# Half of the mixer's projection weight sums by adding loads; the reciprocal of the counts and the last operand halves at other places

## The chip, the cores and the metric

The kernel runs on one core of one Trainium2 chip. The metric is the device time of one execution in microseconds (us); a time for a kernel is the median of several runs. Profiles are of one execution each. Engines: PE is TensorE's matmul, PEld its weight load, DVE is VectorE, ACT is ScalarE, POOL is GpSimd, and SP is the sync engine, which here only issues DMAs.

## The reference: what is computed

One layer of a hybrid encoder on x (2048 positions, 1024 channels), all in float32:

```python
xn = rmsnorm(x, norm1_g)
u_pool, zq, zf, zi, zo, zg = split(xn @ w_in)           # 512 each, gates 2 x 1024
gates = sigmoid(zg + b_gate)
ya = pool_mixer(u_pool, pool_w, pool_scale) @ w_pa      # trailing means over 2, 4, 8, 16 positions
yb = hgrn2_mixer(zq, zf, zi, zo, lower_bounds, hgrn_norm_g) @ w_pb   # gated recurrence, 4 heads
x = x + (gates[0] * ya + gates[1] * yb) @ w_o
x = x + conv_glu_ffn(rmsnorm(x, norm2_g), w_up, conv_w, conv_b, w_down)
out = rmsnorm(x, final_g)
```

`pool_mixer` divides a window's sum by min(position, window), the count; only the first 16 positions have counts below the window.

## The kernel before

**Products.** Every large matrix product is done by a seven-product scheme (Strassen-Winograd) on 2 x 2 blocks: seven block products P1 to P7 instead of eight. The 2048 positions are worked in two superblocks of 1024 (b0 = 0 and 2, each two blocks of 512 positions), and a superblock's two halves are one of the 2 x 2 directions. The operand made of activations is called a form: B11, B21, T2, T1, T3, T4, B22 for P1, P2, P6, P5, P7, P4, P3. The operand made of weights is a quarter of the weight tile or a sum of quarters: P1, P2 and P4 take quarters 0, 1 and 3 as they are; P5 takes s1 = q2 + q3, P6 takes s2 = s1 + q0, P7 takes s3 = q2 + q0, and P3 takes s4 = s2 + q1 (signs are folded into the layout). Each float32 operand is split into a high part, rounded to fp32r by ACT (L231 for weights, L658 for forms), and the rest, taken by DVE (L232, L659). Three matmuls, high x high, high x low and low x high, give a product, so each P of a unit is 4 x 3 = 12 matmuls of 128 x 128 by 512 columns (L148).

**Stages of a superblock.** (1) The io stage, `proj_io`: the hgrn inputs zi and output gates zo, in the order P1, P2, P6, P5, P7, P4, P3 (products io_X to io_V; DVE's io_u of L1316 subtracts after P7 and lets P4 go on in the same PSUM bank). (2) The column projections: 14 units (`PROJ`: four fq for q and forget logits, two u for the pooling channels, eight g for the gates), each in the order P1, P6, P5, P7, P2, P4, P3. Beside them run the pool tasks and, three at a time, the hgrn tasks, whose matmuls (`pl`, `pk`, `pv`, `po`, `pt`) lie between those of the units on PE. In an hgrn task's double levels POOL copies a part of the operand (L1012), and DVE's product of L1016 reads it. (3) The branch projections pa and pb, then wo. (4) The feed-forward part, `ffn`: up (22 units), then dn.

**The weight stream.** `stream` is a list of raw loads and a list of conversions made in advance for the whole kernel. `load` (L197, SP) brings 128 x 512 floats (256 KB) into one of 8 raw buffers; `load_ahead` goes on while the buffer of eight loads ago has had its last conversion, strictly in order, and it stops at a load whose source does not exist yet. `convert` makes the two parts in one of 6 operand buffers, at most LOOKAHEAD = 4 products ahead of PE. A raw load may have a second source, `plus`, that is added on its way in: three ticks after the load (a tick is 6 large matmuls), or at the conversion if that comes first, POOL issues an adding DMA onto the same buffer (L165). It can start only when the load has landed.

**Who makes the weight sums.** In the first superblock's io stage: P5 and P6 on DVE, P7 as a load with an added load, and P3 as a load of the kept P6 sum with q1 added. For the 14 projection units of the first superblock: all four on POOL (`comb`, L444), two additions at P6, one at P7, one at P3. `keep` writes each sum to DRAM (L341, SP), and the second superblock loads them there. For wo, up and dn a background task (`prepare`) adds whole groups from DRAM to DRAM (L304, POOL; L307, ACT).

**The order of the work.** The kernel is written as tasks that are stepped every tick. A planner then orders each engine's instructions by priority (the order in which the program gives them) and by when its own simulated timeline says that they are ready; engines run their lists in order and wait at each instruction for its inputs. `behind(a, b)` holds a behind b in one engine's list. `in_turn` does so for matmuls outside the stream.

**What the change touches.** `weights_of_unit` (L433), which plans the POOL sums. `setup_task` (L601), begun at P7 of the first io stage: it makes masks on POOL, waits for the eighth adding load (`added[7]`), makes the 4 x 16 counts on POOL (L637, L641) and takes their reciprocal on DVE (L643). `forms_b_task` (L793), which makes the forms T1 to T4 and B22 of a superblock's second half; for the feed-forward part (`src[0] == "m"`) its last loop makes the four B22 halves one a tick, with the stream's lookahead at 3 instead of 4 until it ends. `mixer` (L1366), which calls `proj_io` and then joins the setup task.

Of the kernel before, what the change touches and what calls it, by code (L numbers as in the profile page):

```python
# [81 lines left out]
def tile_trunk(  # L82
# [60 lines left out]
    def join(task):  # L143
        while task.live:
            task.step()
# [22 lines left out]
    class Stream:  # L168
# [11 lines left out]
        def raw(self, src, plus=None):  # L180
            r = Raw(src, plus)
            self.raws.append(r)
            return r
# [96 lines left out]
    stream = Stream()  # L280
# [51 lines left out]
    def keep(key, t, later=False):  # L332

        nm = "kw" + "".join(str(c) for c in np.ravel(key[1])) + f"{key[0]}{key[2]}"
        kept[key] = dram.tile([P, 512], F32, tag=nm, name=nm)
        keeping.append((kept[key], t, later))
# [96 lines left out]
    def weights_of_unit(src_v, src_g, unit):  # L433
        src = quarters(src_v, src_g)
        raws, tmp = {}, {}

        def raw(i):
            if i not in raws:
                raws[i] = stream.raw(src[i])
            return raws[i]  # L440

        def comb(nm, key, x0, x1):
            t = slot(f"{nm}{key}")
            pool.tensor_tensor(t, x0, x1, ALU.add)  # L444
            tmp[key] = t
            keep(("in", unit, key), t)
            return t

        def plan(p):
            if p == "P5":  # L450
                return (lambda nm: tmp["s1"]), []
            rs = [raw(i) for i in {"P1": (0,), "P2": (1,), "P4": (3,), "P6": (0, 2, 3),
                                   "P7": (0, 2), "P3": (1,)}[p]]

            def fn(nm):
                t = [r.tile for r in rs]
                if p == "P6":
                    comb(nm, "s1", t[1], t[2])
                    return comb(nm, "s2", tmp["s1"], t[0])
                if p == "P7":  # L460
                    return comb(nm, "s3", t[1], t[0])
                if p == "P3":
                    return comb(nm, "s4", tmp["s2"], t[0])
                return t[0]

            return fn, rs

        return {p: (lambda p=p: plan(p)) for p in ORDER}
# [132 lines left out]
    def setup_task():  # L601
        scratch = [hist.rearrange("p a b -> p (a b)")[:, :64], uhist.rearrange("p a b -> p (a b)")]

        def mask_of():
            scratch.reverse()
            return scratch[0]

        keys = [(h, h, 0, h) for h in (1, 2, 4, 16)]
        keys += [(8 * h + t, 2 * h, t * h, h) for h in (4, 16) for t in range(2)]
        for key, x, off, w in keys:  # L610
            nb = 64 // x
            mf = mask_of()
            behind(pool.memset(mf, 1.0), last_root[0] if len(masks) < 6 else added[3])
            v = mf.rearrange("p (b h) -> p b h", h=x)
            pool.affine_select(out=v, in_=v, pattern=[[-2 * x, nb], [0, x]],
                               compare_op=ALU.is_ge, fill=0.0, base=-off, channel_multiplier=1)
            pool.affine_select(out=v, in_=v, pattern=[[2 * x, nb], [0, x]],
                               compare_op=ALU.is_ge, fill=0.0, base=off + w - 1,
                               channel_multiplier=-1)
            m8 = const.tile([P, 64], U8, tag=f"m{key}", name=f"m{key}")  # L620
            yield 2
            pool.tensor_copy(m8, mf)
            masks[key] = m8.rearrange("p (b h) -> p b h", h=x)
        for t in range(2):
            mf = mask_of()
            behind(pool.memset(mf, 0.0), added[3])
            pool.affine_select(out=mf, in_=mf, compare_op=ALU.not_equal, fill=1.0, base=-t,
                               pattern=[[-2, 64]], channel_multiplier=1)
            m8 = const.tile([P, 64], U8, tag=f"md{t}", name=f"md{t}")
            yield 2  # L630
            pool.tensor_copy(m8, mf)
            masks[-1 - t] = m8.unsqueeze(1)
        pool.memset(hist, 0.0)
        pool.memset(uhist, 0.0)
        while len(added) < 8:
            yield 1
        ins = pool.iota(inv[:, 3], pattern=[[1, 16]], base=1, channel_multiplier=0,  # L637
                        allow_small_or_imprecise_dtypes=True)
        behind(ins, added[7])
        for g, w in enumerate(WINDOWS):  # L640
            pool.tensor_scalar(inv[:, g], inv[:, 3], float(w), None, ALU.min)  # L641
        flat_inv = inv.rearrange("p a b -> p (a b)")
        dve.reciprocal(flat_inv, flat_inv)  # L643
        for h in range(HEADS):
            pool.memset(state[h, 0], 0.0)

# [146 lines left out]
    def forms_b_task(src, gain, forms, full, after, go, early):  # L793
# [94 lines left out]
        while len(forms["B22"]) < 4:  # L888
# [4 lines left out]
            if early:  # L893
# [6 lines left out]
                        else:  # L900
                            stream.convert()
                stream.stop = 26 + k if k < 2 else None
            yield 1
        stream.room = LOOKAHEAD

    x2d = {}
# [461 lines left out]
    def mixer(b0, forms, late):  # L1368
# [5 lines left out]
        proj_io(b0, forms, late, vd, zd)  # L1374
        if b0 == 0:
            join(setup[0])
            prep.append(Task(prepare()))


# [497 lines left out]
```

## Time and profile before

| what | value |
|---|---|
| median of 3 runs | 2542.44 us (2541.99 to 2544.25) |
| the profiled execution, time | 2540.99 us |
| its span, first to last instruction | 2539.3 us |
| mean granted clock of PE | 0.998 |
| DMA | 493.75 MB moved, mean 194 GB/s |
| conversions of weights, ACT L231 | 744, 620 ns each |
| conversions of weights, DVE L232 | 744, 749 ns each |

The profiled execution's own time is 1.45 us under the median of the runs. In the profile a group's line names the line of the kernel, the engine, the operation, what it writes and reads, the shapes and the count. A wait names the engine and line that waited, and what ended the wait. In a timeline row the first number is the start in us from the first instruction, the second the time that it took; neighbouring instructions of one kind are merged (x2), and brackets give the engine's idle time before it and what ended that.

### The profile page before, as it was taken

What the parts mean: (1) busy time and instruction counts of PE and PEld (TensorE: products, weight loads), DVE (VectorE), ACT (ScalarE), POOL (GpSimd) and SP (SyncE); (2) the same over time, 40 slices, a digit from 0 to 9 for tenths busy, and PEclk for the clock granted to TensorE, in tenths of its full rate; (3) what the DMA queues carried; (4) which work ended last, traced back from release to release, by engine and by line L of the source; (5) the groups of instructions that cost most, each with busy time, mean ns of one, the idle gap of its engine ahead of it and who ended that gap; (6) DMA issues with size and microseconds to landing.
All of it is one profiled execution on the core that took longest, in us unless ns stands there. A gap on an engine that the chain in (4) does not pass through costs nothing.

```text
span 2539.3 us, 35647 instructions
## 1 busy us (share of the span) xinstructions
PE 2511.9 (99%) x11508; PEld 2054.1 (81%) x11508; DVE 1979.2 (78%) x3508; ACT 1176.5 (46%) x2218; POOL 752.6 (30%) x1127
## 2 busy tenths in 40 slices
PE   9999999999999999999999999999999999999998
PEld 7788887788788888888888888888887888888886
DVE  7799778498999777885586778765979888778755
ACT  6434434334545444554554343442355544445534
POOL 4334343002344334461230212200033432325410
PEclk9999999999999999999999999999999999999999
DMA  8787777767898889997444343447443454447952
GB/s 274 241 200 220 201 212 227 228 214 242 209 246 240 221 233 242 264 364 243 133 146 150 107 135 109 137 150 224 149 154 110 153 154 136 150 137 236 327 165 97
DMA packets 252331, 493.75 MB, mean 194 GB/s; under 512 B 26544, under 2 KB 43056, under 8 KB 251824
## 3 DMA queue, kind: packets, MB, share of 16 engines
q1 hardware_dynamic: 184512, 313.60, 39.1%
q0 software_dynamic: 42656, 112.74, 17.6%
q10 hardware_dynamic: 24976, 65.13, 7.5%
q8 instruction: 91, 1.49, 0.3%
q14 instruction: 96, 0.79, 0.1%
HBM read 381.79 MB, written 187.17 MB: 224 GB/s over the span
## 4 chain that ended last, share of the span: by engine, by line
PE 90%; DVE 6%; issue 1%; DMA 1%; ACT 1%; POOL 0%; SPq 0%; DVEq 0%; POOLq 0%; ACTq 0%
PE dn_P L148 16%; PE up_Z L148 14%; PE up_X L148 10%; PE up_V L148 9%; PE wo_P L148 6%; PE gr_Z L148 4%; PE pb L148 4%; PE pa L148 3%; PE gr_X L148 3%; PE gr_V L148 3%; PE fr_Z L148 2%; PE io_Z L148 2%; PE fr_X L148 2%; PE fr_V L148 2%; PE io_V L148 1%
## 5 line engine op out<-in xcount | busy, mean ns | idle before, releaser
L231 ACT CAST ops<-raw 128x512 fp32r<-128x512 f32 x744 | 459.7, 620 | 823.1 <-PE dn_P L148 180.5
L232 DVE TENSOR_TENSOR ops<-raw,ops 128x512 fp32r<-128x512 f32 x744 | 554.5, 749 | 218.3 <-ACT ops L231 210.3
L1613 DVE SCALAR_TENSOR_TENSOR e<-h,cols,e 128x512 f32<-128x512 f32 x176 | 143.6, 819 | 31.2 <-ACT e L1611 24.2
L1611 ACT ACTIVATE e<-h,cols 128x512 f32<-128x512 f32 x176 | 142.6, 814 | 25.6 <-DVE h L1160 18.9
L1616 DVE SCALAR_TENSOR_TENSOR e<-h,cols,e 128x512 f32<-128x512 f32 x176 | 134.0, 770 | 2.7
L962 POOL DMA_DIRECT2D g_P<-dg_P x154 | 84.0, 547 | 159.7 <-PE dn_P L148 113.3
L1270 POOL TENSOR_TENSOR gf_P<-e,e 128x512 f32<-128x512 f32 x44 | 62.2, 1415 | 149.6 <-DVE e L1622 93.0
L1270 POOL TENSOR_TENSOR gf_P<-gf_P,e 128x512 f32<-128x512 f32 x44 | 59.0, 1341 | 72.1 <-DVE e L1622 71.6
L1606 POOL COPY h<-h 128x2 f32<-128x2 f32 x88 | 40.9, 476 | 125.0 <-DVE h L1159 118.2
L1408 POOL TENSOR_TENSOR q<-q,qs 128x512 f32<-128x512 f32 x16 | 21.7, 1358 | 187.4 <-ACT qs L1407 180.8
L1445 ACT ACTIVATE gt<-gt,cols 128x512 f32<-128x512 f32 x48 | 34.8, 725 | 85.9 <-DVE gt L1160 61.3
L1620 ACT ACTIVATE e<-e 128x512 f32<-128x512 f32 x88 | 55.6, 631 | 39.8 <-DVE e L1616 39.4
L1608 POOL COPY hist<-h 128x2 f32<-128x2 f32 x88 | 37.8, 429 | 116.6 <-DVE h L1160 114.8
L1160 DVE TENSOR_TENSOR h<-up_u,up_V 128x512 f32<-128x512 f32 x88 | 60.1, 683 | 11.3 <-PE up_V L148 10.8
L1245 DVE TENSOR_TENSOR x<-x,wo_P 128x512 f32<-128x512 f32 x88 | 56.1, 683 | 12.0 <-PE wo_P L148 11.8
L1245 DVE TENSOR_TENSOR ac<-ac,dn_P 128x512 f32<-128x512 f32 x72 | 47.1, 682 | 16.8 <-PE dn_P L148 16.6
L1012 POOL COPY qm<-q 128x64 f32<-128x64 f32 x64 | 27.1, 452 | 99.0 <-issue 26.2
L1027 PE MATMUL pl<-qm,k 128*128 128x192 f32 x256 | 50.6, 327 | 3.7 <-DVE k L1048 3.6
L1636 POOL DMA_DIRECT2D dg_P<-gf_P x88 | 50.8, 577 | 8.3 <-POOL gf_P L1270 7.4
L1195 ACT COPY up_e<-up_X 128x512 f32<-128x512 f32 x44 | 25.8, 586 | 57.8 <-PE up_X L148 52.7
L1606 POOL COPY h<-hist 128x2 f32<-128x2 f32 x88 | 46.0, 530 | 20.6 <-issue 20.6
L1027 PEld LDWEIGHTS pl<-qm,k 128*128 128x128 f32 x256 | 43.9, 189 | 9.6 <-POOL u L926 2.3
(1285 smaller groups left out, 8088.4 us busy)
## 6 DMA issues: line engine op xcount, KB each, us to landing
g_P<-dg_P POOLq DMA_DIRECT2D x154, 256.0 KB, 6.0
raw<-in_w_up_t SPq DMA_DIRECT2D x132, 256.0 KB, 3.2
raw<-in_w_in_t SPq DMA_DIRECT2D x98, 256.0 KB, 3.3
dg_P<-gf_P POOLq DMA_DIRECT2D x88, 256.0 KB, 4.0
dg_P<-e SPq DMA_DIRECT2D x66, 256.0 KB, 3.8
raw<-in_w_dn SPq DMA_DIRECT2D x66, 256.0 KB, 3.7
x<-in_x SPq DMA_DIRECT2D x64, 256.0 KB, 4.9
gd<-gt ACTq DMA_DIRECT2D x64, 256.0 KB, 3.1
```

The source lines that it names most:

```text
L148: count[1] = pe.matmul(*args, **kw)
L231: self.mark = act.copy(hi, v)
L232: low = self.low = dve.tensor_tensor(lo, v, f32(hi), ALU.subtract)
L962: eng.dma_start(t, d)
L1027: ins = pe.matmul(pa_[:, c * 192 : c * 192 + 192], ks[:, (i + c) * P : (i + c + 1) * P], mv[:, c].rearrange("p s x -> p (s x)"), start=Tru ...
L1160: return dve.tensor_tensor(dst, t, ps, ALU.add if how == "add" else ALU.subtract)
L1245: dve.tensor_tensor(t, t, ps[j], ALU.add if sg > 0 else ALU.subtract)
L1270: pin(eng.tensor_tensor(t, x0, x1, op))
L1606: pool.tensor_copy(h[:, 0:2], hist[:, mt] if hf == 0 else hs[s, 0][:, TB : TB + 2])
L1611: in_turn(act.activation(t, h[:, 2:], AF.Identity, bias=col(o_cb + mt), scale=col(o_cw + 4 * MF + mt)))
L1613: in_turn(second(dve.scalar_tensor_tensor(t, h[:, 1 : 1 + TB], col(o_cw + 2 * MF + mt), t, ALU.mult, ALU.add)))
L1616: dve.scalar_tensor_tensor(t, h[:, 0:TB], col(o_cw + mt), t, ALU.mult, ALU.add)
```

## The change

Three edits.

1. For the 14 projection units of the first superblock, s3 (P7) becomes a load of quarter 2 with quarter 0 added on its way in, and s4 (P3) a load of the s2 that was kept in DRAM, with quarter 1 added. s1 and s2 stay on POOL. The two sums are still kept in DRAM, now from the raw buffer and behind the conversion. A unit then has six raw loads instead of four.
2. The reciprocal of the counts leaves the setup task and is issued by `mixer` after the io stage, behind the last conversion's low part.
3. For the feed-forward part, the last B22 halves are issued without a tick between them.

```diff
@@ weights_of_unit
         def plan(p):
             if p == "P5":
                 return (lambda nm: tmp["s1"]), []
-            rs = [raw(i) for i in {"P1": (0,), "P2": (1,), "P4": (3,), "P6": (0, 2, 3),
-                                   "P7": (0, 2), "P3": (1,)}[p]]
+            if p == "P7":
+                rs = [stream.raw(src[2], src[0])]
+            elif p == "P3":
+                rs = [stream.raw(lambda: kept.get(("in", unit, "s2")), src[1])]
+            else:
+                rs = [raw(i) for i in {"P1": (0,), "P2": (1,), "P4": (3,), "P6": (0, 2, 3)}[p]]
 
             def fn(nm):
                 t = [r.tile for r in rs]
                 if p == "P6":
                     comb(nm, "s1", t[1], t[2])
                     return comb(nm, "s2", tmp["s1"], t[0])
-                if p == "P7":
-                    return comb(nm, "s3", t[1], t[0])
-                if p == "P3":
-                    return comb(nm, "s4", tmp["s2"], t[0])
+                if p in SUM_OF:
+                    keep(("in", unit, SUM_OF[p]), t[0], True)
                 return t[0]
@@ setup_task
         for g, w in enumerate(WINDOWS):
             pool.tensor_scalar(inv[:, g], inv[:, 3], float(w), None, ALU.min)
-        flat_inv = inv.rearrange("p a b -> p (a b)")
-        dve.reciprocal(flat_inv, flat_inv)
         for h in range(HEADS):
             pool.memset(state[h, 0], 0.0)
@@ forms_b_task, the loop over the last B22 halves
                 stream.stop = 26 + k if k < 2 else None
-            yield 1
+            if src[0] != "m":
+                yield 1
         stream.room = LOOKAHEAD
@@ mixer
         proj_io(b0, forms, late, vd, zd)
         if b0 == 0:
             join(setup[0])
+            flat_inv = inv.rearrange("p a b -> p (a b)")
+            behind(dve.reciprocal(flat_inv, flat_inv), stream.low)
             prep.append(Task(prepare()))
```

## The prediction

> **What bounds the kernel now.** I read the first line of the page, then the list of PE's waits, then the busy time by stage, then the stretches in which PE stands.
>
> ```profile
> PE 2511.9 (99%) x11508; PEld 2054.1 (81%) x11508; DVE 1979.2 (78%) x3508; ACT 1176.5 (46%) x2218; POOL 752.6 (30%) x1127
> ```
>
> PE is busy for all but 27.4 us of the 2539.3 us span (2539.3 - 2511.9), so a change that alters no matmul can only win idle PE time and matmuls run at a low clock. The waits of PE (total us, times, longest) say which idle time is not start-up:
>
> ```profile
> PE pl L1027 <- DVE k L1048: 3.6, 2, 1.9
> PE io_Z L148 <- DVE io_u L1316: 3.0, 1, 3.0
> PE pt L1145 <- DVE ot L1139: 1.8, 1, 1.8
> PE up_V L148 <- DVE m_B223l L659: 1.8, 2, 0.9
> ```
>
> All are waits for DVE. Next the same work in both superblocks: the column projections with their hgrn tasks (first and third row) and the first branch projection (second row). The columns are the window, then PE, PEld, DVE, ACT, POOL busy with instruction counts, granted clock, DMA share, GB/s.
>
> ```profile
> 103.00:461.00 358.00, 351.59 (x1777) 292.24 (x1776) 300.00 (x678) 142.71 (x319) 138.38 (x150) 1.00 0.78 217
> 461.00:507.00 46.00, 44.16 (x195) 35.49 (x195) 20.27 (x37) 12.84 (x29) 2.39 (x3) 1.00 0.77 239
> 1366.00:1712.00 346.00, 345.93 (x1764) 290.29 (x1763) 257.58 (x664) 142.99 (x317) 58.82 (x86) 1.00 0.43 128
> ```
>
> In the first superblock PE idles 358.00 - 351.59 = 6.4 us and then 46.00 - 44.16 = 1.8 us, 8.2 us together; in the second it idles 0.07 us. DVE is busy 300.0 against 257.6 us for nearly the same count: 42.4 us more. POOL is busy 138.4 against 58.8, and only the first makes weight sums. So three places can pay: the io stage (3.0 us and what follows it), the two B22 stalls (1.8), the first superblock's mixer (8.2).
>
> **Part 1: the reciprocal leaves the io stage.** DVE, then POOL, around it:
>
> ```profile
> 74.64 0.69 DVE L1316 TENSOR_TENSOR io_u<-io_Z,io_e 128x512 f32<-128x512 f32 x1 [2.60 <-PE io_Z L148]
> 78.56 0.55 DVE L643 RECIPROCAL inv<-inv 128x64 f32<-128x64 f32 x1 [3.23 <-POOL inv L641]
> 79.03 1.82 DVE L1316 TENSOR_TENSOR io_u<-io_Z,io_e 128x512 f32<-128x512 f32 x3
> 80.77 0.68 DVE L659 TENSOR_TENSOR x_T41l<-x_t,x_T41h 128x512 fp32r<-128x512 f32 x1
> 81.37 0.68 DVE L865 TENSOR_TENSOR x_t<-x_b,x_t 128x512 f32<-128x512 f32 x1
> 81.97 0.68 DVE L232 TENSOR_TENSOR ops<-raw,ops 128x512 fp32r<-128x512 f32 x1
> ```
>
> ```profile
> 75.28 1.75 POOL L165 DMA_DIRECT2D raw<-in_w_io  x2 [5.11 <-DMA raw<-kw2ioP]
> 76.68 0.53 POOL L637 IOTA inv<- 128x16 f32 x1
> 77.29 1.24 POOL L641 TENSOR_SCALAR inv<-inv 128x16 f32<-128x16 f32 x4
> ```
>
> POOL waits 5.11 us for a load, issues two adding loads, and only then makes the counts. The reciprocal waits for them in DVE's order, and three io_u subtractions wait behind it; PE's T4 matmuls of rows 1 to 3 wait for those. The stall is followed by matmuls at a low clock; first PE alone (window, busy, clock, DMA), then a piece of the chain of waits at full clock:
>
> ```profile
> 79.70:83.40 3.70, 3.69 (x9) 0.54 0.16 28
> ```
>
> ```profile
> 551.28 44.40 PE wo_P L148 x192
> ```
>
> At full clock a matmul takes 44.40 / 192 = 0.231 us, nine take 2.1, so 3.70 - 2.1 = 1.6 us more are lost. Without the reciprocal, io_u of row 1 follows at 75.3 and the others as PE ends each row, some 0.7 us apart, the last to about 77.4; then the three instructions that now span 80.77 to 82.65 take 1.9 us, to 79.2. PE, starting T4 at 75.84 with twelve matmuls at 0.231 us, wants the last of them (the low half of the second weight tile) at about 78.9: what is late next is that one, 0.3 us. **Term: 3.0 + 1.6 - 0.3 = 4.3 us gained** (bounds 2 and 4.6: at the low end DVE's next chain gives some back). At its new place behind the io stage the 0.55 us lie on DVE in front of nothing that is due, for the first use is in the pool tasks; without that cover they cost 0.55. Nothing is due on POOL for the iota either.
>
> The Trainium skill, "TensorE: Matmul & The Clock Gate" (Part 1, "What's actually happening"), lets the clock fall after an idle window of about 3.4 us. By that page of the Trainium skill a gap of 3.0 us need not bring the half speed, the 1.6 us would stay, and the sum would be 1.6 smaller. The rows of the stages around it stand at 1.00 and 0.54 begins at the end of this gap, so here the gap is the cause and I keep the 1.6.
>
> **Part 2: the B22 halves.** DVE in the first superblock's up stage:
>
> ```profile
> 678.56 0.69 DVE L659 TENSOR_TENSOR m_B220l<-m_b,m_B220h 128x512 fp32r<-128x512 f32 x1
> ...
> 683.50 0.69 DVE L659 TENSOR_TENSOR m_B223l<-m_b,m_B223h 128x512 fp32r<-128x512 f32 x1
> ```
>
> Spread over ticks, the four take from 678.56 to 684.19. Put in a row they take 4 x 0.6 us at DVE's pace and end near 681, and B223l is wanted some 0.9 us before 684.2: the cover is 2 us. What moves behind them is a conversion, an h and an e by up to 1.8 us, and the conversions run two or more products (2.8 us each) ahead. The lookahead also returns to 4 sooner. **Term: 2 x 0.9 = 1.8 us gained** (0 if the planner, which orders by priority and readiness, leaves them where they are; 2.3 with the pipeline's refill of about 0.2 a stall).
>
> **Part 3: P7 and P3 sums by adding loads.** 14 units lose two POOL additions each, 28 of these 56 (the window's busy time of that line on POOL):
>
> ```profile
> 87.00:440.00 353.00, 81.08 (x56) 1.00 0.79 221
> ```
>
> One takes 81.08 / 56 = 1.45 us, so POOL loses 28 x 1.45 = 40.5 us. A POOL addition also holds DVE:
>
> ```profile
> 88.55 1.68 POOL L444 TENSOR_TENSOR w29s<-raw,raw 128x512 f32<-128x512 f32 x1 [10.02 <-DVE z L1160]
> ```
>
> ```profile
> 88.98 1.79 DVE L659 TENSOR_TENSOR x_B220l<-x_b,x_B220h 128x512 fp32r<-128x512 f32 x1
> ```
>
> Beside it a DVE subtraction takes 1.79 instead of 0.68 us. By the stage rows the 51 additions that fall behind 103 us cost DVE 42.4 us, 0.83 each; 26 of the removed ones lie there, so DVE gets back 26 x 0.83 = 21.6 us, half of its excess. PE's 8.2 us are all lateness of DVE, and I let them fall in proportion: 4.2 us gained (bounds 0 and 8.2).
>
> Added are 28 adding loads on POOL, 28 more 256 KB loads on SP and, for P3, a trip through DRAM; the stores of the sums are as many as before. What an adding load costs is shown by the eight of the io stage (issue on POOL: min/median/max ns, and issue to landing in us):
>
> ```profile
> L165 POOL DMA_DIRECT2D raw<-in_w_io x8: 858/866/1249, 40.5 to 76.1; - x8
> ...
> DMA to landing us min/median/max: 4.1/5.8/8.4
> ```
>
> Issue: 28 x 0.87 = 24.4 us on POOL, less than the 40.5 that go. The waits are what can hurt. The trip of a P3 sum, as the io stage has it: store, load behind the store's landing (SP), add behind the load's (POOL).
>
> ```profile
> 61.37 0.38 SPq L341 DMA_DIRECT2D kw1ioP<-raw  x1
> 65.56 0.32 SPq L197 DMA_DIRECT2D raw<-kw1ioP  x1
> ```
>
> ```profile
> 69.31 0.86 POOL L165 DMA_DIRECT2D raw<-in_w_io  x1 [3.06 <-DVE ops L232]
> ```
>
> From 61.37 to 69.31 and 5.8 us of landing: 13.7 us, and 1.3 for the conversion: 15. Against that stands the room from the end of s2 on POOL to PE's first use of P3. The shortest of the 14 units is g 0:
>
> ```profile
> 117.67 1.29 POOL L444 TENSOR_TENSOR w36s<-w36s,raw 128x512 f32<-128x512 f32 x1
> ```
>
> ```profile
> 142.70 0.40 PE L148 MATMUL gr_V<-x_B220h,ops 128*128 128x512 f32 x1
> ```
>
> 142.70 - 118.96 = 23.7 us, so the median trip fits with 8 us over. The slow one, from this window's landings, does not leave any:
>
> ```profile
> raw<-in_w_in_t SPq DMA_DIRECT2D x48, 256.0 KB, 4.5
> ...
> kwg7ins<-w121s SPq DMA_DIRECT2D x2, 256.0 KB, 8.7
> ```
>
> 8.7 + 4.5 + 0.9 + 8.4 + 1.3 = 23.8. While SP waits for a store's landing (4.2 us above), the next unit's loads stand behind it; with six loads a unit instead of four, the eight buffers hold 1.3 units ahead, not 2. While POOL waits for a load's landing (3.06 and 5.11 us above), its copies for the hgrn levels stand behind it, and DVE stops at the product that reads them. One such pair:
>
> ```profile
> 139.71 0.42 POOL L1012 COPY qm<-q 128x64 f32<-128x64 f32 x2 [2.84 <-DVE gt L1160]
> ```
>
> ```profile
> 145.46 0.29 DVE L1016 TENSOR_TENSOR qm<-qm,f 128x128 f32<-128x128 f32 x1
> ```
>
> Room 145.46 - 140.13 = 5.3 us, against a hold of 3.06 to 5.11. So the new waits cost PE between nothing and, if both adds of a unit hold POOL in a row, 14 x (2 x 4.1 - 5.3) = 41 us. I take 1.0, near the lower end, since a single hold fits in the room shown and a P3 trip in the 23.7. DMA: 14 units x 4 x 0.262 MB = 14.7 MB over 358 us is 41 GB/s on top of 217; the third stage row shows 128 for the like work, so load times here are already those of a busy window. **Term: 4.2 - 1.0 = 3.2 us gained.**
>
> **Sum.** 4.3 + 1.8 + 3.2 = 9.3 us off the profiled execution's 2540.99 (its span is 2539.3): 2531.7. The runs' median, 2542.44, lies 1.45 above that execution, so 2533.1; I say 2533.
>
> **Rivals.** *(a) The mixer becomes like the second superblock's.* Half the additions are enough for DVE to catch up and all 8.2 us go, with nothing added: 2542.4 - 4.6 - 2.3 - 8.2 = 2527. For it: the second superblock's DVE still spends 257.6 of 346 us and PE idles 0.07. Against: the P6 additions stay, two in a row for each unit, and with them half of DVE's excess.
>
> *(b) SP's queue eats the relief.* Each P3 load holds SP for a store's landing, the loads behind it come later, conversions come late, and ACT and DVE, in order, with them. If this costs 0.7 us a unit, 14 x 0.7 = 9.8, less 4.2 of relief, the mixer loses 5.6 and the change ends at 2542.4 - 6.1 + 5.6 = 2542. For it: the slow trip of 23.8 against 23.7. Against: the median trip is 15, and the room of 23.7 is the shortest of 14.
>
> *(c) Slower: POOL held at landings.* The two adds of a unit wait one behind the other, 2 x 4.1 us, on landings that the plan took as earlier; the copies behind them pass their room of 5.3 and DVE stops. If half of the 14 units meet copies due then: 7 x 2.9 = 20 us, less 6.1, with the relief used up: 2556. It decides from 14 x 0.8 = 11.2 us of new PE waits on (6.1 gained elsewhere plus 0.2%, 5.1). For it: the 5.11 above. Against: it needs a coincidence that the 40.5 - 24.4 = 16 us freed on POOL make rarer.
>
> The Trainium skill, "SBUF — State Buffer" ("SBUF: two separate sides"), warns that descriptors of a GpSimd DMA cannot be written while VectorE runs a two-port instruction. By that page of the Trainium skill (c) would be likelier, for DVE is 84% busy here. The eight rows at 858 to 1249 ns, issued between DVE's subtractions, show at most 0.4 us of it, so I leave the chance of (c) as it is.
>
> **Chances.** Forecast 0.54, (a) 0.15, (b) 0.18, (c) 0.13. A measurement of this kernel tells 0.2%, 5.1 us, from no change. Faster by more: forecast and (a), 0.69; within: (b), 0.18; slower: (c), 0.13. The range reaches from (a) with all bounds, 2526, over (b) to where (c) begins to bite, 2545, and leaves out most of (c) and a little of each edge.
>
> **What would show it.** Right: no wait of PE for io_u over 0.5 us, clock 1.00 there, and the reciprocal behind the io stage; no wait of up_V for m_B223l; 28 additions at L444's place and 36 adding loads in all; DVE busy some 20 us less from 103 to 461; PE idle there below 5 us. Wrong: PE waits for pl or pt grow and DVE's idle time before the qm products names POOL (c); ACT's conversions wait for adding loads, or SP waits for kept stores, with PE waiting for ops (b). The prediction fails if the planner, with other readiness times, moves instructions elsewhere enough to make new stalls beyond the mixer, of which no row here tells.

## The result, and the profile after

The changed kernel takes 2553.31 us (median of 6 runs, 2548.20 to 2558.03), the kernel before 2542.90 beside it (2541.99 to 2544.25): ratio 1.004, 95% interval 1.0027 to 1.0053. It is slower by 10.4 us, where 9.4 us faster was forecast. The profiled execution took 2555.71 us with a span of 2554.0.

First the page's line of busy time, then PE's list of waits, of the changed kernel (total us, times, longest):

```profile
PE 2519.4 (99%) x11508; PEld 2061.3 (81%) x11508; DVE 1956.4 (77%) x3508; ACT 1176.2 (46%) x2218; POOL 728.0 (29%) x1127
```

```profile
PE gr_Z L148 <- DVE gr_u L1198: 8.8, 2, 5.7
PE pl L1028 <- DVE at L1039: 3.8, 2, 2.9
PE gr_Z L148 <- DVE gr_u L1202: 2.6, 2, 2.0
PE pt L1146 <- DVE ot L1140: 2.4, 1, 2.4
```

The waits for io_u and for m_B223l are gone, so two parts of the change did what they were to do. The new waits are all in the first superblock's mixer. PE is idle for 34.6 us instead of 27.4, and it is also busy 7.5 us longer for the same matmuls. Between the first matmuls of the stages in PE's timeline (io_X, fr_X, pb, up_X, dn_P) and the end lie, in us:

| kernel | io stage | mixer | pb to up | up stage | rest |
|---|---|---|---|---|---|
| before | 88.9 | 403.7 | 126.0 | 427.5 | 1479.1 |
| changed | 84.1 | 429.2 | 125.9 | 425.4 | 1475.6 |

The io stage gained 4.8 us, the up stage 2.1, the rest 3.5; the mixer lost 25.5. The mixer's window, first of before, then of the changed kernel (columns as in the prediction):

```profile
103.00:507.00 404.00, 395.74 (x1971) 327.73 (x1970) 320.26 (x714) 155.54 (x347) 140.78 (x153) 1.00 0.78 220
```

```profile
98.00:527.00 429.00, 406.91 (x1969) 334.68 (x1968) 296.86 (x715) 155.83 (x346) 126.54 (x155) 0.97 0.88 242
```

PE's idle time there grew from 404.00 - 395.74 = 8.3 us to 429.00 - 406.91 = 22.1, by 13.8; its busy time grew by 11.2 at a clock of 0.97. DVE did get its relief: 320.26 - 296.86 = 23.4 us less busy time. Who waited instead, in the changed kernel's mixer, is in the list of waits from 84 to 520 us and, for SP's queue, in its own:

```profile
DVE ops L232 <- ACT ops L231: 47.9, 18, 7.4
ACT ops L231 <- DMA raw<-in_w_in_t: 46.5, 10, 7.9
...
POOL raw L165 <- DMA raw<-in_w_in_t: 30.7, 7, 6.6
```

```profile
SPq L341 <- DMA raw<-in_w_in_t: 74.6, 21, 12.3
```

ACT's conversions stand 46.5 us for adding loads. Laid beside the order of the products, 45.6 of these us are at P3 and 0.9 at P7. One such stop, in unit g 3, on POOL, SP, POOL again, ACT, DVE and PE of the changed kernel:

```profile
273.62 1.27 POOL L444 TENSOR_TENSOR w79s<-w79s,raw 128x512 f32<-128x512 f32 x1
...
280.17 0.89 POOL L165 DMA_DIRECT2D raw<-in_w_in_t  x1 [1.64 <-DMA raw<-kwg3ins]
```

```profile
274.92 0.32 SPq L341 DMA_DIRECT2D kwg3ins<-w79s  x1
276.95 0.32 SPq L197 DMA_DIRECT2D raw<-kwg3ins  x1
```

```profile
294.25 0.62 ACT L231 CAST ops<-raw 128x512 fp32r<-128x512 f32 x1 [6.74 <-DMA raw<-in_w_in_t]
```

```profile
294.90 0.69 DVE L232 TENSOR_TENSOR ops<-raw,ops 128x512 fp32r<-128x512 f32 x1 [6.23 <-ACT ops L231]
...
297.64 0.68 DVE L1198 TENSOR_TENSOR gr_u<-gr_e,gr_Z 128x512 f32<-128x512 f32 x1
```

```profile
298.37 0.80 PE L148 MATMUL gr_Z<-x_T30h,ops 128*128 128x512 f32 x1 [5.72 <-DVE gr_u L1198]
298.96 0.63 PE L148 MATMUL gr_Z<-x_T30l,ops 128*128 128x512 f32 x1
299.39 0.63 PE L148 MATMUL gr_Z<-x_T30h,ops 128*128 128x512 f32 x1
...
312.54 0.48 PE L148 MATMUL gr_V<-x_B220h,ops 128*128 128x512 f32 x1
```

POOL ends s2 at 274.9; the store, the load behind it and the add behind that take until 294.2, when ACT goes on: 19.3 us, of which 14.0 are the adding load's own, from its issue at 280.17 to its landing. PE wants the operand that was waited for only at 312.54, 18 us later. But the conversion stands in ACT's order at 287.5, 12.6 us behind the end of s2; ACT stands there for 6.74 us, DVE's low part behind it for 6.23, and an evacuation of another product (gr_u) stands behind that in DVE's order. For this evacuation PE waits 5.72 us. The matmuls that follow come 0.43 us apart (298.96 to 299.39) instead of 0.231.

### The profile page after: what moved, and what is told of

The parts are those of the page before. It is cut to its first block, busy times and chain, and to the rows that moved or that the text cites. A ratio compares the mean times of both kernels' runs of the same rounds, so it can differ in the third digit from the quotient of the medians.

```text
span 2554.0 us, 35779 instructions
## 1 busy us (share of the span) xinstructions
PE 2519.4 (99%) x11508; PEld 2061.3 (81%) x11508; DVE 1956.4 (77%) x3508; ACT 1176.2 (46%) x2218; POOL 728.0 (29%) x1127
## 4 chain that ended last, share of the span: by engine, by line
PE 90%; DMA 4%; DVE 3%; ACT 1%; issue 1%; POOL 1%; SPq 0%; ACTq 0%; POOLq 0%; DVEq 0%
PE dn_P L148 16%; PE up_Z L148 14%; PE up_V L148 10%; PE up_X L148 10%; PE wo_P L148 6%; PE gr_Z L148 4%; PE pb L148 3%; PE pa L148 3%; DMA raw<-in_w_in_t 3%; PE gr_X L148 3%; PE io_Z L148 3%; PE gr_V L148 2%; PE fr_Z L148 2%; PE io_V L148 2%; PE pl L1028 1%; PE fr_X L148 1%
## 5 line engine op out<-in xcount | busy, mean ns | idle before, releaser
L231 ACT CAST ops<-raw 128x512 fp32r<-128x512 f32 x772 | 476.2, 620 | 888.1 <-PE dn_P L148 178.2
L232 DVE TENSOR_TENSOR ops<-raw,ops 128x512 fp32r<-128x512 f32 x772 | 572.7, 745 | 247.1 <-ACT ops L231 239.4
L1411 POOL TENSOR_TENSOR q<-q,qs 128x512 f32<-128x512 f32 x16 | 21.7, 1354 | 185.1 <-ACT qs L1410 185.1
L1161 DVE TENSOR_TENSOR h<-up_u,up_V 128x512 f32<-128x512 f32 x88 | 60.1, 683 | 10.4 <-PE up_V L148 10.0
L165 POOL DMA_DIRECT2D raw<-in_w_in_t x28 | 25.2, 900 | 117.7 <-DMA raw<-in_w_in_t 30.7
```

The source lines that it names most:

```text
L231: self.mark = act.copy(hi, v)
L232: low = self.low = dve.tensor_tensor(lo, v, f32(hi), ALU.subtract)
L1161: return dve.tensor_tensor(dst, t, ps, ALU.add if how == "add" else ALU.subtract)
```

## The experiments

Theories. **A**: P3's way through memory ends after the place of its conversion in ACT's order; ACT, DVE and PE then stop one behind the other. **B**: the 28 adding loads cost by their traffic and holds. **C**: SP stands at the kept stores, so later loads are late. Later came **C'**: POOL stands at adding loads and its own mixer work is late (the prediction's rival (c)), and **D**: a sum made in a raw buffer holds it through its kept store. Medians below have five or more runs, those of e5 and e7 four; ratios are to the kernel before beside them, with a 95% interval in brackets. The diffs show the lines that matter. A profile is of one execution, and some lie far from their median: e10's took 2550.72 us (median 2543.56), e14's 2532.70 (2538.22), e16's 2540.53 (2545.67). Lengths of the mixer from these three are weak evidence; the medians decide.

### One part at a time

e1: the changed kernel with all four sums on POOL again.

```diff
-            if p == "P7":
-                rs = [stream.raw(src[2], src[0])]
-            elif p == "P3":
-                rs = [stream.raw(lambda: kept.get(("in", unit, "s2")), src[1])]
+            rs = [raw(i) for i in {..., "P7": (0, 2), "P3": (1,)}[p]]
```

> The reciprocal's and the B22 halves' new places alone; all four weight sums stay on POOL. Theory A (the loss is all in the P3 sums): 4.3 and 1.8 us under before, 2536 to 2538. Theory B (the 28 adding loads' traffic and holds): the same 2536 to 2538, since there are none. If the two moves are themselves bad (the planner's new order), it lies above 2543. PE should not wait for io_u and m_B223l.

2533.59 us, ratio 0.9963 (0.9950 to 0.9975), 2.4 under the range; mixer 403.7 us as before. The two moves gain 10.0 us by the medians and 7.5 between the two profiled spans, where 6.1 was forecast. The loss is the sums' alone.

e2 and e3: e1 with only s3 (P7), and with only s4 (P3), as an adding load.

> As the changed kernel, but the P3 sums are made on POOL again: 14 adding loads, for P7 alone. Theory A (P3's trip through DRAM ends late and ACT, in order, stops at its conversion): none of the loss is left, 2531 to 2537, and ACT waits for adding loads under 3 us in all. Theory B (28 adding loads load DMA and hold POOL): half of the loss is left, about 2545.

> As the changed kernel, but the P7 sums are made on POOL again: 14 adding loads, for P3 alone. Theory A: nearly the whole loss stays, 2549 to 2556, with 35 us or more of ACT's waits for adding loads. Theory B: half of it stays, about 2545.

e2: 2529.22, ratio 0.9945 (0.9932 to 0.9957), mixer 401.2, faster than either theory said. e3: 2555.71, ratio 1.0046 (1.0033 to 1.0059), mixer 432.4. The same number of adding loads gains 4.4 us on e1 in one place and costs 22.1 in the other. Traffic is not what parts them, for both make the same number of loads, adds and stores and move 501.2 MB in all. In the window from 98 to 500 us, e2 and then e3, PE gets through 1837 instructions in e3 against 1973, and the DMA engines are no busier (0.82 against 0.85):

```profile
98.00:500.00 402.00, 395.26 (x1973) 328.04 (x1972) 308.12 (x713) 156.19 (x346) 138.15 (x155) 1.00 0.85 240
```

```profile
98.00:500.00 402.00, 377.81 (x1837) 312.15 (x1836) 297.46 (x699) 149.09 (x336) 135.52 (x155) 0.96 0.82 227
```

The waits of the two, e2 and then e3:

```profile
POOL raw L165 <- DMA raw<-in_w_in_t: 40.5, 8, 9.5
...
ACT ops L231 <- DMA raw<-in_w_in_t: 0.2, 1, 0.2
```

```profile
ACT ops L231 <- DMA raw<-in_w_in_t: 43.8, 8, 8.3
```

POOL stands 40.5 us in e2, ACT 43.8 in e3. PE feels little of POOL's stand. Of its two waits over 1 us in e2's mixer one leads back to it: 1.6 us for a q of DVE, which waited for a product of POOL behind a stand of 5.82 us. The expectations of e13 and e16, which say that PE waits for none of it, are wrong there:

```profile
PE pl L1069 <- DVE q L988: 1.6, 1, 1.6
```

```profile
120.23 0.88 POOL L165 DMA_DIRECT2D raw<-in_w_in_t  x1 [5.82 <-DMA raw<-in_w_in_t]
```

### Traffic by itself: two that failed

e4: e1 with 28 loads and adds that nobody reads. e5: e1 with 28 spare copies and adds in memory.

```diff
+            if p in ("P7", "P3"):
+                stream.raw(src[2], src[0])          # e4
+                    sp.dma_start(spare[n % 4], src[2])                            # e5
+                    pool.dma_start(spare[4 + n % 4], src[0], accum_op=ALU.add)    # e5
```

> Both moves, all sums on POOL, and in every projection unit of the first superblock two more loads with an added load that nothing reads (28 in all): traffic, POOL's issues and holds, and the shorter lookahead of the eight buffers, without a conversion that waits and without a kept store. Theory A: within 3 us of the kernel without them, 2537 to 2540. Theory B: the loss of the changed kernel returns, 2550 or more.

> Both moves, all sums on POOL, and at each P6 of the first superblock's projections two 256 KB copies issued by SP and two 256 KB adding DMAs issued by POOL from the weights to spare DRAM blocks (28 of each), which wait for nothing in practice and which nothing reads: traffic and issue time alone. Theory A (P3's trip ends after the place that its conversion has in ACT's order): within 4 us of the same kernel without them (2533.6), up to 2538. Theory B (DMA traffic and issues): 2550 or more.

e4: 2597.61, ratio 1.0208 (1.0194 to 1.0222). It does not measure traffic: a buffer that nobody converts is loaded again as soon as its turn comes, so the next load waits for the add to land, SP and POOL stand, and the mixer takes 470.7 us. The waits of e4 on POOL and on SP's queue:

```profile
POOL raw L165 <- DMA raw<-in_w_in_t: 130.5, 19, 15.0
```

```profile
SPq L197 <- DMA raw<-in_w_in_t: 168.8, 26, 14.1
```

e5: 2578.56, ratio 1.0137 (1.0122 to 1.0152). The planner issued the spare transfers in the first 115 us. Of the 46.0 us between the spans of e5 and e1, 42.7 lie in the io stage and ahead of it, so e5 says little on the mixer.

### The way through memory

e6 adds q1 in place onto s2's tile, without the load of the kept s2; the add still waits for s2's store. e7 issues the kept stores of s3 and s4 from ACT's queue, so that SP is free. e8 converts P3 only when PE is within two products of it.

```diff
+                tmp["added"] = pool.dma_start(tmp["s2"], src[1], accum_op=ALU.add)   # e6
+                with tc.issue_after(stream.mark.ins):                                # e7
+                    act.dma_start(d, t)
+                if j in late_ops and j >= self.next + 2:                             # e8
+                    return
```

> P7 as in the changed kernel; the P3 sum is made by adding quarter 1 in place onto the s2 tile that POOL made, without the load of the kept s2 (the adding DMA waits for the store of s2 and for P6's conversion). Theory A: the trip loses its load (4 to 5 us of some 19) and SP loses a wait, so most of the loss goes: 2530 to 2540, ACT's waits for the adds below 20 us. Theory B: 14 loads fewer, a quarter of the loss goes, about 2549. Theory C (SP stands at the kept stores): the kept stores are as before, so 2548 to 2553.

> The changed kernel with the kept stores of s3 and s4 issued by ACT behind the conversion instead of by SP. Theory C (SP stands 75 us at these stores, loads come late, and with them the adds): most of the loss goes, 2532 to 2542, and ACT's waits for adds fall below 20 us. Theory A: SP's waits go, but ACT still reaches P3's conversion before its add has landed, 2548 to 2556.

> The changed kernel, but a P3 conversion of the first superblock's units is given to the planner only when PE is within two products of it, not four. Theory A in the form that it is the place in ACT's order that costs, not the sum's lateness for PE: ACT's waits for adds fall below 20 us and the loss shrinks, 2535 to 2546. If P3's sum is late for PE itself, it gets no better, 2550 or more, with waits of the V products for ACT or DVE conversions.

e6: 2544.02, ratio 1.0003 (0.9993 to 1.0013), mixer 419.0. e7: 2559.97, ratio 1.0061 (1.0046 to 1.0076). e8: 2556.25, ratio 1.0047 (1.0031 to 1.0064). In e7 the wait of SP's queue for adding loads fell from 74.6 to 17.5 us (the first row), while ACT's stayed at 46.7 (the second, of the same kernel):

```profile
SPq L345 <- DMA raw<-in_w_in_t: 17.5, 5, 8.3
```

```profile
ACT ops L231 <- DMA raw<-in_w_in_t: 46.7, 9, 8.9
```

The time did not fall with it: C falls. e7 does not move the hold of the prediction's rival (b), where SP waits at P3's load for s2's store to land. Against (b) stands the list of ACT's waits in the changed kernel: the 46.5 us are all at adding loads, and none at a plain load that came late behind such a hold. e8 leaves A where it was, because the stream is converted in order and the next unit's s2 then starts later too; ACT's stops rose to 66.1 us. e6 lies between the ranges of its three theories. It gains 9.3 us on the changed kernel, though ACT still stops some 52 us for P3's sums by the same reading. So the sum of ACT's stops is no measure of the loss. That only those cost behind which something is due is inferred, not shown.

e9 leaves the trip out: P3's load adds w1 to w2 and needs no sum, so `load_ahead` no longer stops at it for a source that does not exist yet. e10 makes s1 and s2 at P1, one product earlier.

```diff
-                rs = [stream.raw(lambda: kept.get(("in", unit, "s2")), src[1])]
+                rs = [stream.raw(src[2], src[1])]                                    # e9
-            {"P1": (0,), ..., "P6": (0, 2, 3)}
+            {"P1": (0, 2, 3), ..., "P6": ()}      # e10: P1 makes s1 and s2, P6 returns s2
```

> This kernel is the changed kernel with one operand replaced: product P3's adding load adds w1 to w2 (both inputs of the program) in place of adding w1 to the kept sum s2, so the output's P3 terms are wrong, while the number and size of loads, adds, kept stores and conversions stay as they are. What goes is only the way of s2 from GpSimd through memory and back ahead of the add. Theory A (the trip through memory ends after the place of P3's conversion in ACT's order): ACT's stops for raw at the conversions fall from 46.5 us to under 5, the mixer's stretch from its first product to the output projection falls from 429 us to 400 to 403, and the time to 2527 to 2532. Theory B (the 14 more adding loads, their traffic and their holds on POOL's and SP's queues cost the time): mixer 420 or more and 2545 to 2553.

> The changed kernel with s1 and s2 made at P1's conversion instead of P6's, one product (about 3.5 us) earlier; all sums as in the changed kernel and both load-added. Theory A: each trip starts about one product earlier against the same place in ACT's order, so ACT's stops for P3's adding loads fall from 46.5 us to 15 to 25 us, the mixer from 429 to 410 to 420 us and the time to 2535 to 2546. Rival: the stops are set by when the DMA engines get to the add (the queues are busy 0.91 of the time there), not by when the trip starts: stops over 40 us and 2550 to 2556.

e9: 2543.91, ratio 1.0004 (0.9995 to 1.0012), mixer 416.1. e10: 2543.56, ratio 1.0001 (0.9992 to 1.0009). ACT's stops for raw fell from 46.5 to 3.1 and 23.7 us. e10's time and stops came out as A said; its mixer, 421.5 us in an execution 7 us above the median, lies just outside. e9 came out as neither theory said: without the trip the time falls by 9.4 us, and 14.7 stay against e2. The theory that the trip was all of it fell here. What PE waits for in e9, and what stood ahead of it on DVE and POOL:

```profile
PE pl L1068 <- DVE q L987: 7.4, 1, 7.4
PE pl L1028 <- DVE qm L1017: 3.8, 2, 2.7
```

```profile
394.38 0.43 DVE L987 TENSOR_TENSOR q<-q,f 128x256 f32<-128x256 f32 x1 [7.91 <-POOL q L1411]
```

```profile
391.70 0.89 POOL L165 DMA_DIRECT2D raw<-in_w_in_t  x1 [12.96 <-DMA raw<-in_w_in_t]
392.29 0.83 POOL L978 MEMSET at<- 128x512 f32 x1
392.78 1.56 POOL L1411 TENSOR_TENSOR q<-q,qs 128x512 f32<-128x512 f32 x1
```

POOL stands 12.96 us at an adding load whose load below has not landed. Its own product for the hgrn task (L1411) stands behind it, DVE waits 7.91 us for that, PE 7.40. That is rival (c)'s mechanism, on another POOL instruction than the copies that it named; the 2.7 us in the second row lead to such a copy. Followed back in the same way, 12.9 us of e9's PE gaps (1.7, 2.7, 1.1 and 7.4) end at POOL standing at an adding load. POOL's stands at adding loads whose load below had not landed add up to some 52 us in the changed kernel (30.7 in its list of waits, 20.9 at loads of the kept s2) and to 96.4 in e9. So part of what e9 still loses came up only when the trip was gone, and the 9.4 us do not measure what the trip costs in the changed kernel.

### Two sums by adding loads without a trip

e11: e2 with s1 as an adding load of two inputs, and s2 and s4 on POOL.

```diff
+            if p == "P6":
+                tmp["r1"] = stream.raw(src[2], src[3])
+                rs.append(tmp["r1"])
```

> The version with P7's sum s3 by adding load and P3's on GpSimd (2529.2) with one sum more by adding load: s1, of w2 and w3, both inputs of the program, so no trip; s2 and s4 stay on GpSimd. Theory A (only a sum that must wait for another sum is bad as an adding load): ACT's stops stay under 10 us, DVE is relieved of some 14 x 0.84 = 11.8 us again, and of that the time takes 0 to 2.5, as it did for s3: 2526.5 to 2529.5. Theory B (each adding load costs by traffic and holds): slower than 2529, 2533 to 2540. A third way: s1's add is wanted by P6, the second product of its unit, whose raw is loaded later than P7's, so its landing (3.9 to 14 us) may come late for ACT: stops of 10 to 30 us and 2533 to 2545.

2554.54, ratio 1.0039 (1.0026 to 1.0052), mixer 426.6: slower than all three expectations. ACT waits for no adding load. It waits for sums on POOL, longest for an s4 (w56s), which stands behind an adding load; e11's waits, then DVE's, then POOL's rows:

```profile
POOL raw L165 <- DMA raw<-in_w_in_t: 47.1, 6, 22.8
...
ACT ops L231 <- POOL w56s L444: 13.4, 1, 13.4
```

```profile
DVE p L947 <- POOL w56s L444: 7.1, 1, 7.1
```

```profile
185.40 0.89 POOL L165 DMA_DIRECT2D raw<-in_w_in_t  x1 [13.01 <-issue]
185.99 1.49 POOL L304 DMA_DIRECT2D su0s<-in_w_up_t  x1
186.65 2.12 POOL L444 TENSOR_TENSOR w56s<-w51s,raw 128x512 f32<-128x512 f32 x1
```

So a second adding load per unit costs without a trip: 14.7 us in e9, 25.3 in e11, against e2.

### Can POOL's stand be taken away?

e12 and e13 issue the mixer's adds 8 ticks after their loads instead of 3, in e9 and in e2.

```diff
-            yield ADD_LAG
+            yield 8 if r.slow else ADD_LAG
```

> The kernel without the trip (P3's load adds w1 to w2, so the output's P3 terms are wrong) with one thing more: in the mixer, GpSimd's adding loads are issued 8 ticks of six matmuls after the load below them instead of 3, about 6.5 us later, so that the load has landed when GpSimd's queue comes to the add. Loads, adds, stores and bytes are the same. Theory C' (GpSimd stands at the adding loads, its copies and sums for the mixer are late, DVE and then PE stop): GpSimd's wait at the adding loads for raw falls from 96.4 us to under 25, the mixer's stretch from 416 to 400 to 404 us, the time from 2543.9 to 2527 to 2533. Theory B (28 adding loads cost by their traffic): mixer 413 or more, 2540 to 2546. If the adds then land too late for ACT, ACT's stops for raw show it (1.7 us without the delay).

> The version with P7's sum alone by adding load (2529.2) with the mixer's adding loads issued 8 ticks after the load below them instead of 3. Its GpSimd stands 40.5 us at these loads, but PE waits for none of it. Theory C': the stand falls under 15 us and the time stays within 2 us, 2527 to 2531, since nothing that stood behind it was late for PE. If the stand costs wherever it is: 2522 to 2526. If the later adds come late for ACT: over 2532, with ACT's stops for raw over 5 us.

e12: 2543.19, ratio 1.0004 (0.9995 to 1.0013). e13: 2528.62, ratio 0.9944 (0.9930 to 0.9958). POOL's stand in e12 fell only to 67.6 us, and in e13 it was 44.0 against 40.5, so neither did what it was to do: the loads themselves are issued late. The trace of e9 shows one reason on SP's queue:

```profile
SPq L197 <- DVE ops L232: 72.3, 27, 8.7
SPq L197 <- DMA kwg6ins<-raw: 15.7, 2, 10.2
SPq L197 <- DMA kwfq3ins<-raw: 15.4, 2, 9.9
```

A raw buffer that holds a sum can be loaded again only when the sum's kept store has landed. POOL's sums lie in slots, of which there are 77; these lie in the ring of 8.

e14 reads those stores from s2's slot instead, in e9; e15 is e14 with the later adds; e16 is e2 with 9 raw buffers and 76 slots; e17 and e18 are e14's edit in the changed kernel and in e10.

```diff
-                    keep(("in", unit, SUM_OF[p]), t[0], True)
+                    keep(("in", unit, SUM_OF[p]), tmp["s2"], True)    # e14, e15, e17, e18
-N_SLOTS = 77
+N_SLOTS = 76                                                          # e16
-N_RAW = 8
+N_RAW = 9                                                             # e16
```

> The kernel without the trip, in which the kept stores of the mixer's s3 and s4 read s2's tile in place of the raw buffer (so the output of P3 in both batches and of P7 in the second is wrong); the stores' number, size and place are the same. A raw buffer is then free after its conversion and not only after its store has landed. Theory D (the ring: a sum made in a raw buffer holds it through its kept store, loads are issued late, GpSimd stands at the adds behind them): SP's waits for kept stores that read raw (some 120 us without this change) go, GpSimd's wait at the adding loads for raw falls from 96.4 us to 30 to 60, the mixer's stretch from 416 to 401 to 408 us, the time from 2543.9 to 2529 to 2536. Theory B (traffic): 2540 to 2546 with the mixer at 412 or more.

> The same with the mixer's adds issued 8 ticks after the load below them instead of 3. Theory D: now load and add come at their own times, GpSimd's wait at the adds for raw falls under 25 us (67.6 with the delay alone), the mixer's stretch is 400 to 404 us and the time 2527 to 2532. Theory B: 2540 to 2546.

> The version with P7's sum alone by adding load (2529.2) with 9 raw buffers in place of 8 and 76 slots in place of 77. Theory D: loads go out earlier and GpSimd's stand at the adds (40.5 us) falls under 30 us, but PE waited for none of it, so 2527 to 2531. Theory B: no change either, 2529, with the stand unchanged. If one slot less stops GpSimd's sums: 2532 to 2540.

> The changed kernel, trip and all, with one edit: the kept stores of the mixer's s3 and s4 read s2's tile in place of the raw buffer (so P3's and P7's operands are wrong in the second batch of positions). Theory D as a cause of its own beside the trip: 4 to 8 us less than the changed kernel's 2553.3, 2545 to 2549, and SP's waits on kept stores that read raw go. If the trip hides the ring (ACT's stop at P3's conversion ends last either way): 2551 to 2555. ACT's stops for raw stay at 35 to 50 us.

> The kernel with s2 made one product earlier (2543.6), with the same edit to the kept stores. Theory D: 4 to 8 us less, 2535.5 to 2540. If e14's gain was the planner's order and not the ring: 2541 to 2546.

e14: 2538.22, ratio 0.9980 (0.9972 to 0.9989). e15: 2538.23, 0.9982 (0.9973 to 0.9991). e16: 2545.67, 1.0006 (0.9995 to 1.0016). e17: 2557.52, 1.0059 (1.0047 to 1.0072). e18: 2540.98, 0.9993 (0.9984 to 1.0001). The edit did its work: SP's waits at loads for kept stores that read raw, summed over its list, are 141.4 us in e9 and 2.3 in e14. e14's window, of the fastest of its eleven executions:

```profile
98.00:500.00 402.00, 391.74 (x1955) 324.52 (x1954) 303.31 (x714) 155.12 (x347) 125.33 (x154) 1.00 0.92 256
```

Without the trip the edit is worth 5.7 us (e14), which misses both ranges. With the early s2 it gains 2.6 (e18) and in the changed kernel it loses 4.2 (e17); there the intervals with and without the edit overlap, so neither is clear of noise. e15 missed: POOL's stand was 65.2 us and not under 25. e14 makes the same transfers as the changed kernel, 508.5 MB in all and here at a higher rate (256 against 242 GB/s), and is 15.1 us faster, so the amount of traffic is not the cause: B falls as the main cause. e16 is the warning on all these pairs: POOL's stand at these loads fell as D said, from 40.5 to 14.6 us, and the time rose by 16.4. Whether the missing slot did that or the new plan that any such edit brings was not separated; ACT waited some 34 us for POOL's sums in e16 and some 20 in e2. So an edit of one buffer weighs as much as the effects looked for.

**Settled**: the loss lies in the mixer's sums; s4 as an adding load with its trip, alone, costs 22.1 us (e3 against e1); s3 as one, alone, goes with a gain of 4.4 (e2 against e1); and a second adding load per unit costs without a trip too (e9, e11). The costs do not add up: the changed kernel, with both, is 24.1 us above e2. **Open**: about 9 us between e14 and e2, and how much of each of these differences is the new plan. POOL still stands 49.4 us at adding loads in e14, but no experiment took that stand away. Best of all are e2 and e13, 0.55% and 0.56% faster than the kernel before.

## Why the prediction was wrong, step by step

**Part 1, the reciprocal**: right. Forecast 4.3 us gained, measured 88.9 - 84.1 = 4.8, just over the upper bound of 4.6; PE has no wait for io_u, and the clock from 79 to 84 us is 1.00. The 0.3 us of lateness that the prediction took off does not show. Keeping the 1.6 us of low clock, against the window of the Trainium skill, was right here.

**Part 2, the B22 halves**: right in kind. Forecast 1.8; the waits are gone, and the up stage is shorter by 2.1 in the changed kernel and by 1.2 in e1, the rest by 3.5 and 1.6. One stall of 0.9 lay in each. What gained beyond the two stalls was not traced.

**Part 3, DVE's relief**: right in DVE's time, not shown in PE's. Forecast 0.83 us of DVE per POOL addition. e1 and e2 differ by 14 of them; the windows 98 to 461 and 461 to 520, e1 first:

```profile
98.00:461.00 363.00, 358.06 (x1809) 297.56 (x1807) 302.15 (x687) 146.56 (x333) 142.61 (x154) 1.00 0.78 219
461.00:520.00 59.00, 57.16 (x244) 45.97 (x242) 31.98 (x54) 13.65 (x23) 0.00 (x0) 0.97 0.74 230
```

```profile
98.00:461.00 363.00, 356.26 (x1801) 296.38 (x1800) 290.34 (x683) 145.52 (x329) 138.15 (x155) 1.00 0.86 239
461.00:520.00 59.00, 59.00 (x261) 47.95 (x260) 34.24 (x58) 14.72 (x25) 0.00 (x0) 1.00 0.77 246
```

302.15 - 290.34 = 11.8 us, 0.84 each. The prediction let PE's idle time fall in proportion: 14 of 26 additions of 4.2 us are 2.3. e2's mixer is 2.5 us shorter than e1's, but that agreement is luck: PE idles 4.9 + 1.8 = 6.8 us in e1 (363.00 - 358.06 and 59.00 - 57.16) and 6.7 in e2. Most of the 2.5 is low clock in e1's second window, about 59 x 0.03 = 1.8 us by an estimate from its 0.97, behind a wait of 1.84 us that e2 does not have. So the relief of DVE is shown, and the 4.2 us that it was to bring PE are not; why e2's median lies 4.4 under e1's stays open.

**Part 3, the new waits**: wrong. The prediction took 1.0 us, "near the lower end, since a single hold fits in the room shown and a P3 trip in the 23.7". The sums cost the mixer 25.5 us net of any relief, so the new waits and the low clock behind them cost that, or some 29 to 30 if the 4.2 is counted as gained. Two steps failed in it. First, the room of 23.7 us was measured to PE's first use of P3. The trip has to end before the conversion's place in ACT's in-order list, which is products earlier; in g 3 there were 12.6 us to that place and 37.6 to PE's use, and the stop cost PE 5.72. Second, the trip was mis-sized. The prediction took 13.7 us up to the landing with the medians of the io stage, 7.9 to the add's issue and 5.8 from there. In the mixer, by the reading shown for g 3, it took 13.0 to 23.3 over the 14 units, mean 18.7: 11.0 to the issue and 7.7 from there. Landings of the adding loads there (min, median, max us) against 4.1/5.8/8.4 in the io stage of before:

```profile
DMA to landing us min/median/max: 3.9/6.3/14.0
```

By the Trainium skill, "DMA: Bandwidth & Descriptors" ("Anatomy of one DMA — SWDGE (gpsimd) path"), a DMA takes about 2.0 us and its bytes at 436 GB/s, an estimate of 2.6 us for 256 KB. Beside the other traffic of this window, at a DMA share of 0.88, no adding load is that quick: the shortest landing is 3.9.

**A term that was left out** is the clock behind new gaps. The prediction priced it in the io stage, but no rival's price had it for the mixer. There it is 11.2 of the 25 us: the windows behind the gaps of 3.08 us (at 214.97) and 5.72 us (at 298.37) in the changed kernel are

```profile
217.00:219.00 2.00, 2.00 (x11) 1.91 (x10) 1.90 (x4) 0.43 (x1) 2.00 (x1) 0.54 0.19 66
298.30:301.00 2.70, 2.63 (x6) 2.15 (x7) 2.66 (x9) 0.43 (x1) 0.00 (x0) 0.50 1.05 230
301.00:304.00 3.00, 3.00 (x12) 2.70 (x11) 0.89 (x2) 0.00 (x0) 0.27 (x1) 0.50 1.07 279
```

**The rivals.** (c) had the right sign and nearly the time, 2556 against 2553, at a chance of 0.13. The time is luck: its mechanism is real (e9, e11), but it is not the first one in the changed kernel. There the PE gaps of 2.0, 5.7, 1.1 and 2.9 us lead back to ACT's stops at P3, and one of 3.1 to POOL. The prediction knew that conversions are late "in order" under (b), and put this down to loads behind a held SP; the stops are at P3's own adding loads. The hold of POOL's DMA issues by DVE, which the prediction weighed for (c), does not show: the 28 issues took 0.86 to 1.27 us, as the eight before did. The bound of 41 us for the new waits did contain the truth, and the value taken was at the wrong end of it.

## What to carry to other kernels

Measure the room for a late operand to the place of the first instruction that waits for it on an in-order engine, and then look at what stands behind that instruction, not at the operand's last consumer. Before a sum goes from an engine to an adding load, ask whether its inputs are ready long before (s3: yes, and it gained) or whether it needs another sum's round trip (s4), and what else stands in the issuing engine's queue. Put the low clock behind new gaps into a rival's price: here it cost nearly as much as the gaps, though not behind each of them. Where every edit plans the instructions anew, trust a difference between two variants only when it is larger than moving one buffer can give: e16 lies 16.4 us off e2.

## What the runs showed of the hardware

A gap of 3.08 us on PE was followed by the half clock in the mixer: 0.54 two us later. After 5.72 us the clock was 0.50 for at least the next 5.7 us, with large matmuls 0.43 us apart. The Trainium skill, "TensorE: Matmul & The Clock Gate" ("Part 1: The HAM clock gate"), has 427 ns for such a matmul at the lower clock, and the trace agrees; it names an idle window of about 3.4 us, and here shorter gaps did it.

The length of one gap does not decide. In the changed kernel the clock fell to 0.62 and then 0.53 behind a gap of 1.07 us (at 385.64) and stayed at 1.00 behind one of 2.04 (at 137.59); in e8 it stayed at 1.00 behind 2.80 us (at 414.28). PE's one long wait for ot (pt <- ot, near the mixer's end) is 1.84 us both in the kernel before and in e1; here are the 2nd to 4th us behind it, before first, then e1:

```profile
474.77:476.77 2.00, 2.00 (x10) 1.62 (x9) 1.20 (x2) 0.00 (x0) 0.00 (x0) 1.00 1.08 298
```

```profile
468.54:470.54 2.00, 2.00 (x6) 1.52 (x6) 0.51 (x1) 0.00 (x0) 0.00 (x0) 0.50 1.07 283
```

What else decides was not tested.

One 256 KB adding load took between 3.9 and 14.0 us from issue to landing within one execution, and its issue on POOL 0.86 to 1.27 us. A POOL addition that leaves gives DVE 0.84 us back, though it takes 1.45 us itself.
